# Memory keys, memory norm and state updates moved to other stages of a decoder step

## The chip, the cores and the metric

The kernel runs on one core of a Trainium2 chip. The metric is the device time of one launch in microseconds (us). An engine is named as in the profile: PE is TensorE's matmul and PEld its weight load, DVE is VectorE, ACT is ScalarE, POOL is GpSimd, and SP is the engine that issues most loads. L1134 is line 1134 of the kernel before.

## The reference, cut to what matters

One decoder layer is run for a prompt of 512 tokens and for a sample group of 8 sequences with 8 new tokens each; the 576 tokens share the weights. All is float32, with a model width of 2048.

```python
h = rms_norm(x, n_pre_mix)
rq, rk, rv, rg, dq, dk, dv = split(h @ w_in)
ret_o, ret_s = retention_chunked(rotate(rq), rotate(rk) * RET_DK ** -0.5, rv, ret_s0)   # S = gamma S + k^T v
diff_o = diff_attend(dq, keys, vals, ...)
mix = concat(silu(rg) * head_rms_norm(ret_o), head_rms_norm(diff_o)) @ w_out
x = x + rms_norm(mix, n_post_mix)
# cross attention: 4 heads of 128 over 256 memory tokens
mem_n = rms_norm(mem_prompt, norm_mem)           # 256 x 2048, prompt group only
mk_p, mv_p = mem_n @ w_xk, mem_n @ w_xv          # the sample group has cached keys and values
x = x + rms_norm(softmax((rms_norm(x, n_pre_x) @ w_xq) @ mk.T / sqrt(128)) @ mv @ w_xo, n_post_x)
h = rms_norm(x, n_pre_ffn)
x = x + rms_norm((silu(h @ w_gate) * (h @ w_up)) @ w_down, n_post_ffn)
```

The outputs are the new x, the new keys and values, the memory keys and values of the prompt, and the updated retention state of every sample (8 heads of 8 times 128 x 128, 4 MB).

## The kernel before

Activations lie transposed: 16 tiles of 128 features by 576 tokens. A float32 product is made of three matmuls in a rounded format: a high and a low part are split off each operand (`split`, L96 to L109: a copy on ACT, a subtraction on DVE), and high*high, high*low and low*high are added in PSUM (`mm3`). Weights come in pieces of 128 x 1024 (512 KB) through a ring of three raw tiles (`wraw`) and are split into rings of two (`wsplit`); products in w_in, w_out and the FFN follow Strassen's scheme over pairs of output blocks and have a second ring of three raw tiles (`w2`, tag wraw2).

The stages follow one another: w_in (8 to 441 us), retention and differential attention, w_out (to 1146), w_xq (1160 to 1215), cross attention (to some 1317), w_xo (to 1375), the FFN. Between w_out and w_xq, and between w_xo and the FFN, stands a norm: the sum of squares over all features is needed before the next operand can be scaled. `bcast_rstd` makes the scale: matmuls with a column of ones (rsb_pr), a root on ACT, a reciprocal and a product with the identity on DVE, matmuls that spread the result over the partitions (rsb_ps), and two copies. `prep_b1` (L1174) then makes each w_xq operand: a product on DVE (L1177), an addition of x by an accumulating DMA from POOL (L1181), a split, a store of the new x, a square and a sum into acc2 (L1189). Its source tiles xr lie in the slots `XS`, that is OAL 0 to 7 and OBH 0 to 7 of a grid of operand slots (7 names by 8 stages, 128 x 576 each).

The order on each engine is not that of the program text: a planner simulates the timeline and gives each engine a fixed queue, in which work that it expects to be ready runs ahead. So loads are hoisted as far as their buffers are free (the first two state loads, L1328, are issued at 1153.7, ahead of the projection). At run time each queue is served in order.

The memory is handled by `prep_mem` (L1131) and `mem_block` (L1146). `prep_mem` loads 16 tiles memT (128 features by 256 memory tokens, 128 KB) into the eight slots of OBL, splits each into a slot of XS as the x tiles there are used up, and squares and sums them (macc) for the memory norm. `mem_block(j)` is one block of 128 output columns: 16 feature tiles by 3 matmuls, 48 in all, then a product with the scale mrs; j 0 to 3 are the keys of the four heads and j 4 to 7 the values, which are also transposed. `cross_sample` works on two samples at a time (scores, softmax, product with the cached values), `cross_prompt(h)` on one head of the prompt, and `state_update(h)` on the retention state of one head: it loads the keys and values kvd (64 KB) and the state (512 KB), spreads the values with a mask (vbd), makes four matmul records (ru), adds on DVE (L1340) and stores. These are called in turn, so that matmul blocks stand between the softmaxes. `prep_bias` (L438) is an earlier example of small work set between two pairs of w_in.

Of the kernel before, what the change touches and what calls it, by code (L numbers as in the profile page):

```python
# [14 lines left out]
F32 = mybir.dt.float32  # L15
F32R = mybir.dt.float32r
# [32 lines left out]
def step_kernel(ctx: ExitStack, tc: tile.TileContext, a: dict, o: dict):  # L49
# [3 lines left out]
    def act(out, in_, func, **kw):  # L53
        S.activation(out, in_, func, **kw)  # L54
# [172 lines left out]
    def opslot(op, st):  # L227
        return op * 8 + st
# [129 lines left out]
    with ExitStack() as pha:  # L358
# [76 lines left out]

        br8d = dp.tile([8, BW], F32, name="br8d")

        def prep_bias():  # L438
            row = e1.w2("brow")[:8, :BW]
            p0, p1 = fb1("bp0"), fb1("bp1")  # L440
            TE.matmul(p0[:8], rb33, ohp[:, :512], start=True, stop=True)
            TE.matmul(p1[:8, : BW - 512], rb33, ohp[:, 512:], start=True, stop=True)
            act(row[:, :512], p0[:8], AF.Copy)
            act(row[:, 512:], p1[:8, : BW - 512], AF.Copy)
            SY.dma_start(br8d, row)
            for h in range(8):
                SY.dma_start(biasd[h], br8d[h : h + 1, :].to_broadcast([P, BW]))
# [676 lines left out]

        return mk

    macc = m0p.tile([P, NMEM], F32, name="macc")
    mrs = m0p.tile([P, NMEM], F32, name="mrs")
    mact = []

    def prep_mem():  # L1131
        for k in range(KT):
            mt = slot(opslot(OBL, k % 8), f"mt{k}")
            SY.dma_start(mt[:, :NMEM], a["memT"][k])  # L1134
            mhl = slot(XS[k], f"mhl{k}", F32R)[:, : 2 * NMEM].rearrange("p (i n) -> p i n", i=2)
            split(mhl[:, 0, :], mhl[:, 1, :], mt[:, :NMEM], gains[:, GMEM + k : GMEM + k + 1])
            mact.append(((mhl[:, 0, :], mhl[:, 1, :]),))
            if k == 0:
                act(macc, mt[:, :NMEM], AF.Square)
            else:  # L1140
                act(mt[:, NMEM : 2 * NMEM], mt[:, :NMEM], AF.Square)
                V.tensor_tensor(macc, macc, mt[:, NMEM : 2 * NMEM], ALU.add)

    mkT, mvn = [], []

    def mem_block(j):  # L1146
        po = pd.tile([P, 2, 512], F32, tag="d", name=f"mem{j}")[:, 0, :NMEM]
        for kh in range(2):
            ws = wload(a["w_mem"][j, kh], f"mem{j}_{kh}")
# [3 lines left out]
        t = m0p.tile([P, NMEM], F32, tag=f"mk{j}" if j < 4 else "mvt", name=f"mkv{j}")  # L1153
        V.tensor_tensor(t, po, mrs, ALU.mult)
        S.dma_start(o["memT"][j], t)
        if j < 4:
            mkT.append(t)
        else:
            pv = bank(f"mvt{j}")
            for i in range(2):  # L1160
                TE.transpose(pv[:, i * P : (i + 1) * P], t[:, i * P : (i + 1) * P], ident)
            vn = m0p.tile([P, NMEM], F32, name=f"mvn{j}")
            act(vn, pv[:, :NMEM], AF.Copy)
            mvn.append(vn)

    def add_dram(y, src, direct):
        if direct:
# [62 lines left out]
    cll = [opslot(op, st) for st in (0, 7) for op in range(4)] + [opslot(OBL, st) for st in range(8)]  # L1230
    cti = [0, 0]

    def cl(name):
# [84 lines left out]
            pt2[:, : 2 * P].rearrange("p (j h t) -> p j h t", j=2, h=XH)[:, :, :, 0:8],  # L1318
        )

    bdm = m0p.tile([NS, NB // 2], F32, name="bdm")
    SY.dma_start(bdm, a["bdm"])

    def state_update(h):
        kv = m0p.tile([NS, 2 * P], F32, tag="kvs", name=f"kvs{h}", bufs=2)
        SY.dma_start(kv, kvd[:, h, :])
        s0 = m0p.tile([P, NB * P], F32, tag="s0", name=f"s0_{h}", bufs=2)
        SY.dma_start(s0, a["state"][h].rearrange("p b v -> p (b v)"))  # L1328
        vbd = m0p.tile([NS, 512], F32, tag="vbd", name=f"vbd{h}", bufs=2)
        V.tensor_tensor(  # L1330
            vbd.rearrange("p (b v) -> p b v", b=4),
            kv[:, P:].unsqueeze(1).to_broadcast([NS, 4, P]),
            bdm.unsqueeze(2).to_broadcast([NS, 4, P]),
            ALU.mult,
        )
        pu = pd.tile([P, 2, 512], F32, tag="d", name=f"ru{h}")
        for g in range(2):
            rows = slice(32 * g, 32 * g + 32)
            TE.matmul(pu[:, g, :], kv[rows, :P], vbd[rows], start=True, stop=True)
        V.scalar_tensor_tensor(  # L1340
            s0, s0, (1.0 - 2.0 ** (-5.0 - h)) ** 8, pu.rearrange("p g n -> p (g n)"), ALU.mult, ALU.add
        )
        S.dma_start(o["rets"][h].rearrange("p b v -> p (b v)"), s0)

    def cross_prompt(h):
        ps = pd.tile([P, 2, 512], F32, tag="d", name=f"xs{h}")
        for qb in range(4):
# [53 lines left out]
    state_update(7)
    dsq = m0p.tile([P, 1], F32, name="dsq")
    act(dsq, epst, AF.Sqrt)
    for h in range(XH):
# [19 lines left out]
    def ydst(j):  # L1424
        yx[j] = slot(yslot[j], f"yx{j}") if j in yslot else w2(f"yx{j}")[:, :T]
        return yx[j]

    mk = post_evac(ydst, acc3, GQX)
    for j in range(KT):
        outs, parts = dpair(f"xo_{j}")  # L1430
        if j % 2 == 0:
            ws = wload(a["w_xo"][j // 2], f"xo{j}")
        for k in range(XH):
            i = (j % 2) * 4 + k
            mm3(outs, (ws[0][:, i, :], ws[1][:, i, :]), oxs[k], k == 0, k == XH - 1)
# [482 lines left out]
```

## Time and profile before

| | |
|---|---|
| time, median of 3 runs | 2946.92 us (2944.44 to 2948.87) |
| the profiled execution | 2941.53 us, its span 2939.5 us |
| busy: PE, DVE, ACT, POOL | 96%, 76%, 45%, 9% of the span |
| DMA | 493.62 MB, 168 GB/s over the span |
| chain that ended last | PE 83%, DMA 7%, DVE 5%, issue 3%, ACT 2% |

Busy time is the share of the span in which an engine had an instruction; matmuls overlap, so a busy PE need not run at its peak. PEclk is the granted TensorE clock, 1.00 being 2.4 GHz and 0.50 being 1.2 GHz. The chain is followed back from the last instruction, at each step to what released it. In a list in order of time, the bracket behind a row says how long the engine stood idle before it and what ended the wait.

### The profile page before, as it was taken

The numbers are of one execution on the slowest core, as the hardware profiler recorded it, in microseconds if no ns is written. First come the engines' busy times: TensorE is split into PE (matmuls) and PEld (weight loads), VectorE is DVE, ScalarE is ACT, GpSimd is POOL, SyncE is SP. The second block draws the span as 40 slices with busy tenths as digits, with TensorE's granted clock in tenths as the row PEclk, the third lists the DMA queues.
The fourth block names the chain that finished last, engine by engine and source line by source line (L and its number), as shares of the span: only waits on it lengthen the run. The fifth ranks groups of instructions, "written<-read, shape, count | busy, mean of one in ns | idle before, by whom it ended". The sixth has DMA issues, their size and how long they took to land.

```text
span 2939.5 us, 54583 instructions
## 1 busy us (share of the span) xinstructions
PE 2809.1 (96%) x22060; PEld 2710.6 (92%) x22060; DVE 2221.1 (76%) x3523; ACT 1333.4 (45%) x2183; POOL 252.9 (9%) x267
## 2 busy tenths in 40 slices
PE   8999998999999998998899999999999999999996
PEld 8899998888878998877799999999999999999995
DVE  8677767556555876864988888888888877888987
ACT  7333344444455645535744444444444444333441
POOL 0000003323332011000100000000000000000004
PEclk9999999999999999999999999999999999999998
DMA  5433336667664536863634444444444466455531
GB/s 166 150 117 126 119 126 240 240 212 256 219 235 163 176 118 214 275 222 96 178 128 140 132 154 133 142 143 137 149 143 131 149 231 228 158 203 207 180 115 65
DMA packets 203351, 493.62 MB, mean 168 GB/s; under 512 B 25907, under 2 KB 68403, under 8 KB 203100
## 3 DMA queue, kind: packets, MB, share of 16 engines
q1 hardware_dynamic: 122588, 334.14, 34.7%
q0 software_dynamic: 22464, 75.38, 8.1%
q10 hardware_dynamic: 58048, 80.63, 7.7%
q8 instruction: 173, 2.83, 0.4%
q14 instruction: 78, 0.64, 0.1%
HBM read 407.07 MB, written 85.61 MB: 168 GB/s over the span
## 4 chain that ended last, share of the span: by engine, by line
PE 83%; DMA 7%; DVE 5%; issue 3%; ACT 2%; POOL 1%; SPq 0%; ACTq 0%; DVEq 0%; POOLq 0%
PE dX L1624 9%; PE Yg L307 7%; PE Yu L307 7%; PE Yin L307 5%; PE Zg L307 5%; PE Xu L307 4%; PE Zu L307 4%; PE Xg L307 4%; PE dZ L1624 4%; PE Xin L307 3%; PE Zin L307 3%; PE rk L118 2%; PE dY L1624 2%; PE Ywo L307 2%; PE rv L118 2%
## 5 line engine op out<-in xcount | busy, mean ns | idle before, releaser
L1624 PE MATMUL dX<-fo,wd 128*128 128x288 f32 x1872 | 271.0, 296 | 4.0 <-ACT ysl L54 4.0
L1624 PEld LDWEIGHTS dX<-fo,wd 128*128 128x128 f32 x1872 | 257.1, 189 | 4.2 <-ACT ysl L54 4.2
L54 ACT ACTIVATE wd<-wr_d 128x512 fp32r<-128x512 f32 x156 | 97.5, 630 | 119.3 <-PE dX L1624 56.7
L1624 PE MATMUL dZ<-fo,wd 128*128 128x288 f32 x936 | 139.2, 294 | 0.0
L1744 POOL TENSOR_TENSOR fin<-fin,ysq 128x320 f32<-128x320 f32 (+1 forms) x10 | 8.4, 839 | 1467.5 <-ACT ysq L54 1467.5
L1624 PEld LDWEIGHTS dZ<-fo,wd 128*128 128x128 f32 x936 | 129.2, 188 | 0.0
L106 DVE TENSOR_TENSOR wd<-wr_d,wd 128x512 fp32r<-128x512 f32 x156 | 106.4, 687 | 12.5 <-ACT wd L54 12.0
L54 ACT ACTIVATE wd<-d 128x512 fp32r<-128x512 f32 x78 | 48.9, 631 | 75.8 <-PE dZ L1624 40.1
L1624 PE MATMUL dY<-fo,wd 128*128 128x288 f32 x468 | 75.5, 295 | 0.0
L698 POOL DMA_INDIRECT vu<-cv,idx x64 | 62.8, 981 | 102.5 <-PE ou L790 62.4
L698 POOL DMA_INDIRECT ku<-ck,idx x64 | 63.7, 996 | 77.5 <-PE su L729 46.7
L54 ACT ACT_TABLE_LOAD x51 | 65.4, 1283 | 9.8 <-DVE ms L1258 2.3
L307 PE MATMUL Xg<-op,wh_p1g 128*128 128x288 f32 x336 | 67.7, 296 | 0.0
L307 PE MATMUL Xu<-op,wh_p1u 128*128 128x288 f32 x336 | 67.6, 296 | 0.0
L1624 PEld LDWEIGHTS dY<-fo,wd 128*128 128x128 f32 x468 | 66.7, 188 | 0.0
L106 DVE TENSOR_TENSOR wd<-d,wd 128x512 fp32r<-128x512 f32 x78 | 53.5, 689 | 9.9 <-ACT wd L54 9.4
L328 DVE TENSOR_TENSOR w_s1g<-w_a21g,wr_a22g 128x1024 f32<-128x1024 f32 x21 | 25.7, 1225 | 40.8 <-DMA w_a21g<-w_gate 40.8
L307 PE MATMUL Yg<-oph,wh_p6g 128*128 128x288 f32 x168 | 50.6, 301 | 5.0 <-ACT oph L54 5.0
L118 PE MATMUL mem<-mhl,wh_mem 128*128 128x256 f32 x256 | 51.5, 298 | 3.1 <-DVE mp L1258 1.9
L307 PEld LDWEIGHTS Xu<-op,wh_p1u 128*128 128x128 f32 x336 | 53.9, 188 | 0.0
L307 PEld LDWEIGHTS Xg<-op,wh_p1g 128*128 128x128 f32 x336 | 53.9, 188 | 0.0
L307 PE MATMUL Xin<-op,wh_p1in 128*128 128x288 f32 x256 | 51.6, 296 | 0.0
(1153 smaller groups left out, 10923.3 us busy)
## 6 DMA issues: line engine op xcount, KB each, us to landing
fo<-fo SPq DMA_DIRECT2D x140, 288.0 KB
wr_d<-w_down SPq DMA_DIRECT2D x39, 512.0 KB
d<-w_down SPq DMA_DIRECT2D x39, 512.0 KB
fo<-sh ACTq DMA_DIRECT2D x60, 288.0 KB
fo<-sl ACTq DMA_DIRECT2D x60, 288.0 KB
w_a21g<-w_gate SPq DMA_DIRECT2D x21, 512.0 KB
wr_a11g<-w_gate SPq DMA_DIRECT2D x21, 512.0 KB
wr_a22g<-w_gate SPq DMA_DIRECT2D x21, 512.0 KB
```

The source lines that it names most:

```text
L54: S.activation(out, in_, func, **kw)
L106: V.tensor_tensor(lo, src, hi.bitcast(F32), ALU.subtract)
L118: TE.matmul(po, ws, x[h][xi], start=start and i == 0, stop=stop and i == 2)
L307: TE.matmul(bk[:, :HN], w[wx][:, st, :], ops[op][st][xi], start=first and st == 0 and i == 0, stop=st == 7 and i == 2, skip_group_check=True,)
L328: V.tensor_tensor(s1, a21, a22, ALU.add)
L698: G.indirect_dma_start(t, None, src, bass.IndirectOffsetOnAxis(ap=idx[:, pg : pg + 1], axis=0))
L1624: TE.matmul(bk[:, :HN], w[wi][:, st, :], ops[e][st][xi], start=start and st == 0 and i == 0, stop=st == 3 and i == 2, skip_group_check=True,)
L1744: (V if j % 2 == 0 or j > 11 else G).tensor_tensor(ac[:, hs], ac[:, hs], sq, ALU.add)
```

## The change

The keys leave `mem_block`. They become a group in eight chunks (`mem_k_chunk`) between w_out and the w_xq projection: each chunk loads 512 KB of weights for two feature tiles and all four heads, two memT tiles, splits both, and adds 24 matmuls into two PSUM banks (kb), which stay taken until two copies (kraw) at the end. The row scale of x (`bcast_rstd`, rsb1) stands between the second and the third chunk. The memT tiles pass through two buffers (tag mt). Their split tiles lie for k 0 to 7 in two tags of two buffers each (b12, tt) and for k 8 to 15 in the slots of OBL, where they stay for the values. For the values, `prep_mem` loads and splits k 0 to 7 a second time: the raw tile into a slot of OBH (`XS[8 + k % 6]`), the split one into OAL.

The squares of the memory norm come from a second, natural copy of the memory in w_in, behind the third pair of blocks: four tiles of 512 KB through the ring `w2`, a square with a running sum on ACT, and root and reciprocal into mstd. `mem_k` spreads it by one product and one matmul and scales the keys.

The state updates leave the cross attention. Heads 0 to 3 stand behind blocks 4, 7, 10 and 13 of w_xo; heads 4 and 5 inside, heads 6 and 7 behind the `bcast_rstd` of the gap behind w_xo. State tiles are halved (256 KB), kvd comes for two heads at a time, and all lie in operand slots. The cached tiles of `cross_sample` rotate over 14 slots (OBH 0 to 5 instead of OBL 0 to 7).

```diff
+        def prep_mem_sums():
+            ms = fa.tile([P, 4], F32, name="ms")
+            for i in range(4):
+                t = e1.w2(f"mn{i}")
+                SY.dma_start(t, a["memN"][i // 2][:, (i % 2) * 1024 : (i % 2 + 1) * 1024])
+                act(t, t, AF.Square, accum_out=ms[:, i : i + 1])
+            msv = ms.rearrange("p (i c) -> p i c", c=2)
+            V.tensor_tensor(mstd, msv[:, :, 0], msv[:, :, 1], ALU.add)
+            act(mstd, mstd, AF.Sqrt, scale=1.0 / D, bias=epst)
+            V.reciprocal(mstd, mstd)
...
+            if n == 2:
+                prep_mem_sums()
...
-    bcast_rstd(acc1, rsb, D, T, "rsb1", fb2)
+    kraw = [slot(opslot(OBH, 6 + i), f"kraw{i}")[:, :512] for i in range(2)]
+    kb = [fb2(f"memk{i}") for i in range(2)]
+    mact = [None] * KT
+
+    def mem_split(k, mt, t):
+        mhl = t[:, : 2 * NMEM].rearrange("p (i n) -> p i n", i=2)
+        split(mhl[:, 0, :], mhl[:, 1, :], mt, gains[:, GMEM + k : GMEM + k + 1])
+        mact[k] = ((mhl[:, 0, :], mhl[:, 1, :]),)
+
+    def mem_k_chunk(c):
+        ws = wload(a["w_mem_g"][c], f"memk{c}")
+        for k in (2 * c, 2 * c + 1):
+            mt = y1p.tile([P, NMEM], F32, tag="mt", name=f"mt{k}", bufs=2)
+            SY.dma_start(mt, a["memT"][k])
+            if k < 8:
+                t = fb.tile([P, T], F32R, tag=("b12", "tt")[k % 2], name=f"mhl{k}", bufs=2)
+            else:
+                t = slot(opslot(OBL, k % 8), f"mhl{k}", F32R)
+            mem_split(k, mt, t)
+        for k in (2 * c, 2 * c + 1):
+            for j in range(4):
+                wi = 2 * j + k % 2
+                for i, (wx, xi) in enumerate(((0, 0), (0, 1), (1, 0))):
+                    TE.matmul(
+                        kb[j // 2][:, (j % 2) * NMEM : (j % 2 + 1) * NMEM],
+                        ws[wx][:, wi, :],
+                        mact[k][0][xi],
...
+    for c in range(KT // 2):
+        if c == 2:
+            bcast_rstd(acc1, rsb, D, T, "rsb1", fb2)
+        mem_k_chunk(c)
+    for i in range(2):
+        act(kraw[i], kb[i], AF.Copy)
     ph2.close()
...
     def prep_mem():
-        for k in range(KT):
-            mt = slot(opslot(OBL, k % 8), f"mt{k}")
-            SY.dma_start(mt[:, :NMEM], a["memT"][k])
-            mhl = slot(XS[k], f"mhl{k}", F32R)[:, : 2 * NMEM].rearrange("p (i n) -> p i n", i=2)
-            split(mhl[:, 0, :], mhl[:, 1, :], mt[:, :NMEM], gains[:, GMEM + k : GMEM + k + 1])
-            mact.append(((mhl[:, 0, :], mhl[:, 1, :]),))
-            if k == 0:
-                act(macc, mt[:, :NMEM], AF.Square)
-            else:
-                act(mt[:, NMEM : 2 * NMEM], mt[:, :NMEM], AF.Square)
-                V.tensor_tensor(macc, macc, mt[:, NMEM : 2 * NMEM], ALU.add)
+        for k in range(8):
+            mt = slot(XS[8 + k % 6], f"mtv{k}")[:, :NMEM]
+            SY.dma_start(mt, a["memT"][k])
+            mem_split(k, mt, slot(XS[k], f"mhlv{k}", F32R))
...
+    mem_k()
     prep_mem()
-    bcast_rstd(macc, mrs, D, NMEM, "mrs")
...
     cross_sample(0)
     cross_sample(2)
-    mem_block(0)
     mem_block(4)
     cross_prompt(0)
-    state_update(0)
     cross_sample(4)
-    mem_block(1)
-    state_update(1)
     mem_block(5)
     cross_prompt(1)
...
+    RS0 = [opslot(op, st) for st in (1, 2, 3) for op in range(5)] + [opslot(OAL, 4)]
+    def state_update(h, bk):
+        if h % 2 == 0:
+            kvt2[0] = slot(opslot(OBL, h // 2), f"kvs{h}")[:NS, :512].rearrange("p (h c) -> p h c", h=2)
+            SY.dma_start(kvt2[0], kvd[:, h : h + 2, :])
+        kv = kvt2[0][:, h % 2, :]
+        vbd = slot(opslot(OBH, h % 4), f"vbd{h}")[:NS, :512]
...
+        for g in range(2):
+            s0 = slot(RS0[2 * h + g], f"s0_{h}_{g}")[:, :512]
+            SY.dma_start(s0, a["state"][h][:, 4 * g : 4 * g + 4, :].rearrange("p b v -> p (b v)"))
+            rows = slice(32 * g, 32 * g + 32)
+            pu = bk(f"ru{h}_{g}")
+            TE.matmul(pu, kv[rows, :P], vbd[rows], start=True, stop=True)
+            V.scalar_tensor_tensor(s0, s0, (1.0 - 2.0 ** (-5.0 - h)) ** 8, pu, ALU.mult, ALU.add)
+            S.dma_start(o["rets"][h][:, 4 * g : 4 * g + 4, :].rearrange("p b v -> p (b v)"), s0)
...
         mk(j)(parts)
+        if j in (4, 7, 10, 13):
+            state_update((j - 4) // 3, bank)
...
+    def fbank_ru(name):
+        if name == "rsb2_ps0":
+            state_update(4, fbank)
+            state_update(5, fbank)
+        return fbank(name)
+
+    bcast_rstd(acc3, rsf, D, T, "rsb2", fbank_ru)
+    state_update(6, fbank)
+    state_update(7, fbank)
```

## Rows read from the trace of the kernel before

**Rows 1.** The page, part 1: engines, busy us over the span.
```profile
PE 2809.1 (96%) x22060; PEld 2710.6 (92%) x22060; DVE 2221.1 (76%) x3523; ACT 1333.4 (45%) x2183; POOL 252.9 (9%) x267
```

**Rows 2.** Busy us by stretch: PE, PEld, DVE, ACT, POOL; granted clock, DMA share, GB/s.
```profile
1146.20:1215.20 69.00, 55.64 (x390) 53.42 (x391) 55.13 (x88) 42.69 (x76) 12.43 (x15) 0.90 0.99 287
1215.20:1317.20 102.00, 92.64 (x743) 75.52 (x742) 67.12 (x113) 43.37 (x97) 0.00 (x0) 0.95 0.68 229
1317.20:1374.90 57.70, 56.05 (x398) 54.26 (x396) 22.27 (x26) 27.05 (x40) 0.00 (x0) 0.97 0.27 91
1374.90:1421.00 46.10, 30.39 (x200) 27.82 (x199) 34.91 (x59) 32.40 (x55) 12.13 (x14) 0.85 0.80 194
```

**Rows 3.** TensorE in order of time, first gap (start, us; in brackets its wait).
```profile
1149.20 1.18 PE L179 MATMUL rsb_pr<-ones,acc 128*96 128x1 f32 x12 [3.00 <-DVE acc L1062]
1153.75 2.29 PE L203 MATMUL rsb_ps<-rsb,ones 96*128 96x288 f32 x4 [3.37 <-DVE rsb L190]
1160.62 1.33 PE L118 MATMUL xq<-h2h,wh_xq 128*128 128x288 f32 x4 [4.57 <-ACT h2h L54]
```

**Rows 4.** Busy times in steps of 2 us, same gap.
```profile
1162.00:1164.00 2.00, 2.00 (x10) 2.00 (x10) 2.00 (x4) 1.14 (x2) 0.67 (x2) 0.50 0.77 175
1164.00:1166.00 2.00, 2.00 (x16) 2.00 (x15) 1.89 (x3) 0.00 (x0) 1.48 (x2) 0.95 0.98 146
```

**Rows 5.** Chain of waits, memory blocks (start, us, what).
```profile
1226.19 5.75 PE mem L118 x47
```

**Rows 6.** State update: its matmuls in the chain, then tiles vbd and s.
```profile
1239.38 1.06 PE ru L1339 x4
...
L1330 DVE TENSOR_TENSOR vbd<-kvs,bdm x8: 682/684/687, 1157.0 to 1306.5; 64x512 f32<-64x512 f32 x8
...
L1340 DVE SCALAR_TENSOR_TENSOR s<-s,ru x8: 1210/1214/1222, 1240.5 to 1318.3; 128x1024 f32<-128x1024 f32 x8
```

**Rows 7.** Tiles mt and wr_mem: instructions (ns least/median/most, first and last start).
```profile
L54 ACT ACTIVATE mhl<-mt,gains x16: 492/494/510, 1169.8 to 1218.6; 128x256 fp32r<-128x256 f32 x16
L109 DVE SCALAR_TENSOR_TENSOR mhl<-mt,gains,mhl x16: 476/480/485, 1173.4 to 1219.2; 128x256 fp32r<-128x256 f32 x16
...
L54 ACT ACTIVATE wh_mem<-wr_mem x16: 1041/1059/1065, 1214.7 to 1302.5; 128x1024 fp32r<-128x1024 f32 x16
L96 DVE TENSOR_TENSOR wl_mem<-wr_mem,wh_mem x16: 1214/1225/1227, 1216.2 to 1303.6; 128x1024 fp32r<-128x1024 f32 x16
```

**Rows 8.** Chain of waits, single loads.
```profile
1186.79 9.30 DMA mt<-memT
...
1215.67 3.30 DMA xvc<-cmv
```

**Rows 9.** SP's issues of memT, and ScalarE's wait for them.
```profile
1147.25 1.70 SPq L1134 DMA_DIRECT2D mt<-memT  x2
...
1153.59 0.76 ACT L54 ACTIVATE mt<-mt 128x256 f32<-128x256 f32 x2 [1.12 <-DMA mt<-memT]
```

**Rows 10.** Chain of waits, w_xo.
```profile
1330.02 44.80 PE xo L118 x334
```

**Rows 11.** VectorE in order of time, behind the projection.
```profile
1217.76 0.75 DVE L1189 TENSOR_TENSOR acc<-acc,xr 128x576 f32<-128x576 f32 x1
...
1231.57 0.19 DVE L1211 COPY xqs<-xq 128x64 f32<-128x64 f32 x1
```

**Rows 12.** TensorE in order of time, cross attention.
```profile
1259.98 0.69 PE L1315 MATMUL yt<-ident,yob 128*128 128x128 f32 x2 [2.33 <-DVE yob L1312]
```

**Rows 13.** All engines in order of time, the gap behind w_xo.
```profile
1378.03 1.15 PE L179 MATMUL rsb_pr<-ones,acc 128*96 128x1 f32 x12 [2.96 <-ACT yx L54]
...
1381.88 2.29 PE L203 MATMUL rsb_ps<-rsf,ones 96*128 96x288 f32 x4 [2.70 <-DVE rsf L190]
...
1389.96 0.61 PE L118 MATMUL gu0a<-op,wh_gu 128*128 128x288 f32 x1 [5.79 <-ACT op L54]
```

**Rows 14.** Busy times by stretch, w_in.
```profile
100.00:120.00 20.00, 17.35 (x109) 15.57 (x108) 7.54 (x7) 6.53 (x9) 0.00 (x0) 0.91 0.53 160
```

More of the change, by code (lines that the diff above doesn't have):

```diff
@@ L69, in step_kernel @@
     SY.dma_start(gains, a["gains"])
+    mstd = cp.tile([P, 2], F32, name="mstd")
     mixd = dp.tile([KT, P, T], F32, name="mixd")
@@ L1125, in post_evac, with mem_k @@
         return mk
-    macc = m0p.tile([P, NMEM], F32, name="macc")
     mrs = m0p.tile([P, NMEM], F32, name="mrs")
-    mact = []
     def prep_mem():
-        for k in range(KT):
-            mt = slot(opslot(OBL, k % 8), f"mt{k}")
-            SY.dma_start(mt[:, :NMEM], a["memT"][k])
-            mhl = slot(XS[k], f"mhl{k}", F32R)[:, : 2 * NMEM].rearrange("p (i n) -> p i n", i=2)
-            split(mhl[:, 0, :], mhl[:, 1, :], mt[:, :NMEM], gains[:, GMEM + k : GMEM + k + 1])
-            mact.append(((mhl[:, 0, :], mhl[:, 1, :]),))
-            if k == 0:
-                act(macc, mt[:, :NMEM], AF.Square)
-            else:
-                act(mt[:, NMEM : 2 * NMEM], mt[:, :NMEM], AF.Square)
-                V.tensor_tensor(macc, macc, mt[:, NMEM : 2 * NMEM], ALU.add)
-    mkT, mvn = [], []
+        for k in range(8):
+            mt = slot(XS[8 + k % 6], f"mtv{k}")[:, :NMEM]
+            SY.dma_start(mt, a["memT"][k])
+            mem_split(k, mt, slot(XS[k], f"mhlv{k}", F32R))
+    mkT, mvn = [], []
+    def mem_k():
+        V.tensor_tensor(
+            mrs.rearrange("p (c j) -> p c j", c=2),
+            ident.unsqueeze(1).to_broadcast([P, 2, P]),
+            mstd.unsqueeze(2).to_broadcast([P, 2, P]),
+            ALU.mult,
+        )
+        pb = bank("mrs_ps")
+        TE.matmul(pb[:, :NMEM], ones, mrs, start=True, stop=True)
+        act(mrs, pb[:, :NMEM], AF.Copy)
+        for j in range(4):
+            t = m0p.tile([P, NMEM], F32, tag=f"mk{j}", name=f"mkv{j}")
+            V.tensor_tensor(t, kraw[j // 2][:, (j % 2) * NMEM : (j % 2 + 1) * NMEM], mrs, ALU.mult)
+            S.dma_start(o["memT"][j], t)
+            mkT.append(t)
     def mem_block(j):
@@ L1148, in mem_block @@
         for kh in range(2):
-            ws = wload(a["w_mem"][j, kh], f"mem{j}_{kh}")
+            ws = wload(a["w_mem"][j - 4, kh], f"mem{j}_{kh}")
             for k8 in range(8):
@@ L1152, in mem_block @@
                 mm3([(po, 0)], (ws[0][:, k8, :], ws[1][:, k8, :]), mact[k], k == 0, k == KT - 1)
-        t = m0p.tile([P, NMEM], F32, tag=f"mk{j}" if j < 4 else "mvt", name=f"mkv{j}")
+        t = m0p.tile([P, NMEM], F32, tag="mvt", name=f"mkv{j}")
         V.tensor_tensor(t, po, mrs, ALU.mult)
         S.dma_start(o["memT"][j], t)
[L1156 to L1164, printed above, removed]
+        pv = bank(f"mvt{j}")
+        for i in range(2):
+            TE.transpose(pv[:, i * P : (i + 1) * P], t[:, i * P : (i + 1) * P], ident)
+        vn = m0p.tile([P, NMEM], F32, name=f"mvn{j}")
+        act(vn, pv[:, :NMEM], AF.Copy)
+        mvn.append(vn)
     def add_dram(y, src, direct):
@@ L1225, in step_kernel @@
     )
+    mem_k()
     prep_mem()
-    bcast_rstd(macc, mrs, D, NMEM, "mrs")
     ctl = [opslot(op, st) for st in (1, 2, 3, 6) for op in range(4)]
-    cll = [opslot(op, st) for st in (0, 7) for op in range(4)] + [opslot(OBL, st) for st in range(8)]
+    cll = [opslot(op, st) for st in (0, 7) for op in range(4)] + [opslot(OBH, st) for st in range(6)]
     cti = [0, 0]
@@ L1319, in cross_sample @@
         )
[L1321 to L1343, printed above, removed]
     def cross_prompt(h):
@@ L1858 @@
     )
+    wk = n["w_xk"][0]
+    A["w_mem_g"] = _wgroup([wk[:, j * P : (j + 1) * P] for j in range(4)], nat)
+    A["memN"] = np.ascontiguousarray(n["mem_prompt"][0].reshape(2, P, D))
     A["w_out"] = _wblocks(n["w_out"][0])
-    A["w_mem"] = _wblocks(np.concatenate([n["w_xk"][0], n["w_xv"][0]], 1))
+    A["w_mem"] = _wblocks(n["w_xv"][0])
     A["w_gate"] = _wblocks(n["w_gate"][0])
```

22 lines of the change are left out of this document (13 added, 9 removed).

## The prediction

> **What bounds the kernel now.** I read the page's busy times first, then the busy times by stretch, then the waits of TensorE one by one, and only then single transfers. TensorE is busy for 2809.1 of 2939.5 us [rows 1], so whatever the change brings has to come out of some 130 us in which it stands idle, or out of stretches at the lower clock. By stretch [rows 2], two pieces between w_out and the first FFN product are poor: from 1146.2 to 1215.2 (gap behind w_out, then the w_xq group) TensorE works 55.6 of 69.0 us at a granted clock of 0.90, and from 1374.9 to 1421.0 (the gap behind w_xo) 30.4 of 46.1 us at 0.85. The cross-attention stretch in between works 92.6 of 102.0 us, and w_xo itself 56.1 of 57.7 us.
>
> The waits say what the first gap is [rows 3]: w_out's products end at 1146.2 (1149.2 less its wait), then TensorE waits 3.0 us for the sum of squares, 3.4 us for the row scale and 4.6 us for the first normed operand; the projection starts at 1160.6. The granted clock falls to its lower level, 0.50 (1.2 GHz), after these waits and is back only in 1164 to 1166 [rows 4], so the first 3.5 us of the projection run at half speed. In the same stretch DMA is the full resource: a mean busy share of 0.99 over 69 us [rows 2]. So the gap is cheap for TensorE work whose operands have been loaded, and a bad place for work that must be loaded there. That is the question of this change.
>
> I make the sum against the profiled execution, 2941.5 us (span 2939.5 and 2.0 around it). The median of the runs shown is 2946.9, 5.4 above; I add that at the end.
>
> **What leaves the cross stretch.** A block of memory keys is 48 matmuls; 47 took 5.75 us [rows 5], 0.122 us each, 5.9 us a block, 23.4 us for four. One state update takes 1.06 us of TensorE [rows 6]. Eight leave this stretch; four go into w_xo, where TensorE has no room (56.1 of 57.7), so they only change place; the other four, 4.2 us, go into the last gap. Together 27.6 us leave. The memory norm's squares and sums leave VectorE and ScalarE there too; I count nothing for that, because TensorE's work is what covers them.
>
> **What the keys cost in their new place.** Eight chunks, 24 matmuls or 2.9 us each. Chunks 0 and 1 can be split before w_out ends: their memT tiles fit the two mt buffers in turn and the w_out queue is light. Chunk 2's memT tiles wait, loaded, for chunk 0's split tiles (two of each tag), so they are split at about 1146.2 + 2.9 + 1.4 = 1150.5. From there on every chunk needs two new memT tiles through the same two buffers: issue, landing, a 0.49 us copy on ScalarE, a 0.48 us subtraction on VectorE [rows 7], and only then the next issue. I call the landing L and put 1.5 us on the rest. The chunk period is L + 1.5, against 2.9 us of matmuls, and SP issues in order, so every load queued behind a waiting memT load waits as well. In before, eight buffers held these tiles, so this ring is new.
>
> L is bounded on both sides by single transfers. Just behind the projection 256 KB landed in 3.30 us; in the loaded projection a memT tile took 9.30 us [rows 8]. Nearer in place: two issued from 1147.3 were used at 1153.6, at most 6.3 us [rows 9]. I take 3.3: while the ring paces SP, SP has little else in flight, and the accumulating x transfers start only behind the row scale. The Trainium skill (DMA: Bandwidth & Descriptors, Anatomy of one DMA — SWDGE path) gives about 2.0 us plus the bytes over 436 GB/s, by which 128 KB is an estimated 2.3 us, and the sum below would come out 5 us lower; the rows here lie above it, and no run shows the loaded case of the new order.
>
> With 3.3 the period is 4.8: the last of five chunks starts at 1150.5 + 24.0 = 1174.5 and ends at 1177.4. The projection is 384 matmuls of 0.133 us (w_xo's steady rate, [rows 10]), 51 us; I let 4 us of it run in the pauses of the ring, on the PSUM banks that the keys don't hold. It then ends at 1224.4 instead of 1215.2: **+9.2**. From below: with the keys dense (23.4) and the scale's own 1.8 us beside them it ends at 1222.3, +7.1. From above: L = 9.3 makes the period 10.8, the keys end at 1207.4, and with 10 us of the projection pulled forward it ends at 1248: +33.
>
> Beside the ring, the rest of this group hides. A chunk's weights take 1.06 us on ScalarE and 1.23 us on VectorE [rows 7] in a ring of two, so they are ready 2.3 us behind the chunk before last, inside the 2.9 us of the chunk between; without that cover (a dense group) it would be some 0.5 us a chunk. The row scale is asked for behind chunk 1, when its sum (acc1, VectorE at 1149) is just there; its matmuls then run between key chunks, and VectorE's and ScalarE's splits, 2.2 and 2.0 us a chunk, can push it back by one instruction, 1.2 us, which is inside the keys' time. The two raw copies at the end are one more ScalarE pass each, before the keys are needed by 20 us; the scale of the keys is now one matmul on a finished column. SP gets eight memT loads more (0.33 us each to issue, 1 MB), behind the xr loads and ahead of the cross-attention tiles; POOL's queue gets nothing.
>
> **A late start of the values.** The change splits k 0 to 7 a second time, and loads mt for k = 5 into the slot of xr 13, which is read until the last sum of acc2. That sum starts at 1217.8, 2.6 us behind the projection [rows 11]. Then come 3.3 us of transfer and 1 us of split: some 7 us, against about 4 us of work (five k of the first value block, the rsx matmuls). In before only the split stood there. **+3**, between 0 and 5.
>
> **Less cover.** Key blocks filled TensorE while the xq scale was made (the last xqs copy is at 1231.6, 16 us behind the projection, [rows 11]) and between softmaxes. Even with eight blocks TensorE waited 2.3 us for VectorE at one place [rows 12]. With four blocks fewer such waits are hidden. Four cross_sample and four cross_prompt chains are left with half the cover; at half a us each: **+4**; 0 if the remaining blocks suffice, 13 if six of them show some 2.2 us each.
>
> **The last gap.** Four updates bring 4 times 0.68 us of VectorE for vbd, which can be made early in w_xo (VectorE 22 of 58 us busy there), and 4 times 1.21 us for the state [rows 6]. Their matmuls fit TensorE's waits of 3.0, 2.7 and 5.8 us [rows 13]. But VectorE runs in order, and the chain to the first FFN matmul runs through it (the row scale, the ym products and sums). Of 4.9 us I put **+1.5** on the path; at best −0.5, as work in the gap keeps the clock up; at worst all 4.9, with 2 MB of state writes beside a stretch that DMA fills to 0.80 [rows 2].
>
> **The memory sums.** Four 512 KB tiles pass through the three-buffer ring that feeds the w_in products, each with a squaring of about 1.06 us. When prep_bias went through there, TensorE worked 17.4 of 20 us [rows 14]. **+1**, between 0 and 4.
>
> Sum: −27.6 + 9.2 + 3 + 4 + 1.5 + 1 = −8.9; 2941.5 − 8.9 = 2932.6, and with 5.4 added 2938.
>
> **Rivals.** (A) The ring decides, slower: L as in the loaded projection, 9.3 us. Then −27.6 + 33 + 3 + 4 + 1.5 + 1 = +15, 2962. It turns from gain to loss where the projection ends 18 us late, at a period of 6.6, L = 5.1; the 6.3 us of [rows 9] lie above that, the 3.3 of [rows 8] below. For it: DMA at 0.99 in this stretch. Against it: SP, held by the ring, can't prefetch cross-attention tiles, which were part of that load.
> (B) Cover, no change: cross attention becomes a chain of softmaxes and gives 13 us back: about 2947. For it the wait in [rows 12]; against it, 92.6 of 102 us busy. That the planner's order puts keys behind the projection after all, so that the gap stays, ends here too.
> (C) The gap fills as meant: dense keys, no late values, no loss elsewhere: −27.6 + 7.1 = −20.5, 2926.
>
> **How the numbers follow.** The forecast (2933 to 2943) has 0.37, C 0.19, B 0.22, A 0.22. A measurement of this kernel can tell about 0.2%, 5.9 us, from no change. Faster by more: most of the forecast, 0.33, and C, 0.19: 0.52. Slower: A less its mild end, and a worse B: 0.22. Within: 0.26. The range, 2922 to 2960, runs from a little below C to just under A's full price, and leaves out about 1 in 10 on either side.
>
> **What would show it.** Right: key matmuls between 1146 and about 1177, a granted clock that stays at 1.0, the projection ending near 1224, w_xo ending some 13 us earlier than 1374.9, the FFN's first matmul about 15 us behind it as before. Wrong: single key chunks 7 us or more apart, each behind a memT landing (A); the cross stretch little shorter than 102 minus 15 us, with TensorE waiting for VectorE (B); a wait of 3 us or more in w_in behind a squaring; the state sums between the scale and ym in the last gap.

## The result, and the profile after

The changed kernel takes 2971.31 us (median of 4 runs, 2968.87 to 2974.14), the kernel before 2946.43 us on the same chip (4 runs, 2944.44 to 2948.87): a ratio of 1.0084, 95% interval 1.0067 to 1.0102. It is **slower by 0.84%**; forecast were 2938 us and a range of 2922 to 2960. The spans of the two profiled executions, 2939.5 and 2967.1 us, differ by 27.6 us, and the stages below are read from these two. A profiled execution can lie some 5 us to either side of its kernel's median (before 5 below it, experiment e1 4 above), so stage differences of 2 or 3 us are not taken for effects.

The page, part 1, answers to [rows 1]: busy us over the span.

```profile
PE 2832.6 (95%) x22056; PEld 2727.7 (92%) x22056; DVE 2219.1 (75%) x3524; ACT 1339.9 (45%) x2188; POOL 252.9 (9%) x267
```

TensorE has four matmuls fewer and is busy for 23 us longer. The same matmuls ran longer: that points to the clock. The same stages as in [rows 2] (keys, projection, cross attention, w_xo, gap and first 32 us of the FFN), columns as there:

```profile
1155.10:1216.00 60.90, 34.67 (x211) 32.05 (x209) 46.63 (x68) 36.80 (x58) 12.42 (x15) 0.75 0.91 242
1216.00:1267.40 51.40, 51.40 (x373) 51.40 (x374) 18.06 (x24) 14.77 (x21) 0.00 (x0) 0.96 0.60 197
1267.40:1337.70 70.30, 60.89 (x514) 47.91 (x512) 38.88 (x74) 30.08 (x74) 0.00 (x0) 0.93 0.54 180
1337.70:1399.40 61.70, 60.76 (x416) 54.80 (x414) 32.27 (x49) 29.83 (x50) 0.00 (x0) 1.00 0.44 148
1399.40:1447.40 48.00, 40.15 (x229) 33.14 (x229) 38.73 (x65) 32.45 (x55) 12.12 (x14) 0.82 0.86 231
```

From the end of w_out to the start of the projection it was 14.4 us (1146.2 to 1160.6); it is now 60.9 us, of which TensorE works 34.7. The projection itself went from 54.6 to 51.4 us, cross attention from 102.0 to 70.3, w_xo (to the end of its last matmul, 1375.1 and 1399.4) from 57.9 to 61.7, the last gap from 15.0 to 16.1 (to the first FFN matmul at 1415.5). What moved out of cross attention did come out. What came in behind w_out costs more than that.

The keys stretch in steps of 5 us, to be held against [rows 4], same columns:

```profile
1165.00:1170.00 5.00, 4.98 (x38) 4.54 (x37) 4.46 (x9) 3.19 (x5) 0.18 (x1) 1.00 0.65 222
1170.00:1175.00 5.00, 1.09 (x8) 0.68 (x6) 5.00 (x8) 3.57 (x8) 0.98 (x1) 1.00 0.60 196
1175.00:1180.00 5.00, 4.31 (x22) 4.10 (x22) 3.05 (x6) 0.99 (x3) 1.77 (x2) 0.66 1.02 234
1180.00:1185.00 5.00, 1.28 (x5) 0.99 (x6) 5.00 (x8) 4.54 (x8) 1.72 (x2) 0.71 1.01 218
...
1190.00:1195.00 5.00, 0.00 (x0) 0.00 (x0) 2.35 (x4) 2.30 (x3) 0.79 (x1) 0.73 1.05 265
1195.00:1200.00 5.00, 3.74 (x15) 3.45 (x16) 4.25 (x7) 3.30 (x6) 1.73 (x2) 0.50 0.79 189
```

Two halves. Up to about 1170.5 four and a half chunks (108 of the 192 key matmuls, nine memT tiles) run dense, at a granted clock of 1.00 in the last full slice. By then the row scale is ready (1168.3), the preparation of x starts (POOL's column is no longer near zero, DMA goes to about 1.0), and TensorE alternates between idle and work; the granted clock of these slices is 0.50 to 0.74, between its two levels or at the lower one.

TensorE's waits from 1100 to 1460 us, by line and releaser (us in all, times, longest), which answer to [rows 3, 12]:

```profile
PE memk L1137 <- ACT mhl L54: 12.5, 4, 6.6
PE memk L1137 <- DVE mhl L110: 7.9, 4, 3.1
PE xq L119 <- ACT kraw L54: 5.8, 1, 5.8
PE xs L1379 <- DVE mkv L1200: 4.3, 1, 4.3
```

The waits of [rows 3] for the row scale and the first operand are gone, as the change set out to do. In their place stand 20.4 us for split memory tiles and 5.8 us for the copy that frees the keys' banks. Which of a tile's steps was late is read from the issues, engine by engine. SP's queue (start, duration):

```profile
1174.90 1.09 SPq L1127 DMA_DIRECT2D mt<-memT  x2
1183.93 0.33 SPq L90 DMA_DIRECT2D wr_xq<-w_xq_g  x1
1184.36 1.36 SPq L1127 DMA_DIRECT2D mt<-memT  x2
1195.97 0.33 SPq L90 DMA_DIRECT2D wr_xq<-w_xq_g  x1
1197.03 0.33 SPq L1127 DMA_DIRECT2D mt<-memT  x1
```

ScalarE's (in brackets its wait and what ended it):

```profile
1179.14 0.77 ACT L54 ACTIVATE h2h<-ym,gains 128x576 fp32r<-128x576 f32 x1 [4.01 <-DMA ym<-xT]
...
1181.34 0.89 ACT L54 ACTIVATE mhl<-mt,gains 128x256 fp32r<-128x256 f32 x2
...
1191.84 0.78 ACT L54 ACTIVATE h2h<-ym,gains 128x576 fp32r<-128x576 f32 x1 [3.39 <-DMA ym<-xT]
...
1195.27 0.51 ACT L54 ACTIVATE mhl<-mt,gains 128x256 fp32r<-128x256 f32 x1 [1.14 <-DMA mt<-memT]
...
1197.21 0.51 ACT L54 ACTIVATE mhl<-mt,gains 128x256 fp32r<-128x256 f32 x1 [1.43 <-DMA mt<-memT]
```

VectorE's subtractions, which end a split and free the buffer:

```profile
1183.82 0.48 DVE L110 SCALAR_TENSOR_TENSOR mhl<-mt,gains,mhl 128x256 fp32r<-128x256 f32 x1
...
1196.53 0.48 DVE L110 SCALAR_TENSOR_TENSOR mhl<-mt,gains,mhl 128x256 fp32r<-128x256 f32 x1
```

And three landings, of the loads issued at 1174.90, 1184.36 and 1185.39 (KB, us from issue to landing):

```profile
mt<-memT SPq DMA_DIRECT2D x1, 128.0 KB, 4.4
...
mt<-memT SPq DMA_DIRECT2D x1, 128.0 KB, 10.9
...
mt<-memT SPq DMA_DIRECT2D x1, 128.0 KB, 11.8
```

Two rounds of the ring, late for two reasons. In the first, a tile issued at 1174.90 lands at 1179.3, but ScalarE copies it only at 1181.34, behind an operand of x that had itself waited 4.01 us for a transfer, and VectorE subtracts at 1183.82; only then can the next load be issued, at 1184.36: 9.5 us, of which the landing is 4.4 and the rest 5.1. In the second, the tile is copied at 1195.27, as soon as it lands, and the next load goes out at 1197.03: 12.7 us, of which the landing is 10.9 and the rest 1.8. With two tiles a round, TensorE begins on them at 1171.9, 1181.9, 1195.8 and 1204.1: periods of 10.0, 13.9 and 8.3 us, 10.7 in the mean, where rival A had 10.8. The transfers issued from 1171 to 1208, behind the row scale (KB each, median us from issue to landing over those whose landing the trace tells, for memT the three above), answering to [rows 8, 9]:

```profile
x1d<-ym ACTq DMA_DIRECT2D x12, 288.0 KB, 5.0
ym<-xT POOLq DMA_DIRECT2D x12, 288.0 KB, 7.2
wr_xq<-w_xq_g SPq DMA_DIRECT2D x4, 512.0 KB
mt<-memT SPq DMA_DIRECT2D x5, 128.0 KB, 10.9
```

and two pieces of the chain that ended last (start, us, what):

```profile
1185.39 11.80 DMA mt<-memT
...
1206.68 7.98 DMA ym<-xT
```

The chain changes between memT and x transfers: neither waits alone.

### The profile page after: what moved, and what is told of

Read it like the earlier page. It is cut to its first block, busy times and chain, and to the rows that moved or that the text cites. A ratio compares the mean times of both kernels' runs of the same rounds, so it can differ in the third digit from the quotient of the medians.

```text
span 2967.1 us, 54638 instructions
## 1 busy us (share of the span) xinstructions
PE 2832.6 (95%) x22056; PEld 2727.7 (92%) x22056; DVE 2219.1 (75%) x3524; ACT 1339.9 (45%) x2188; POOL 252.9 (9%) x267
## 4 chain that ended last, share of the span: by engine, by line
PE 83%; DMA 6%; DVE 5%; issue 3%; ACT 2%; POOL 1%; SPq 0%; ACTq 0%; DVEq 0%; POOLq 0%
PE dX L1679 9%; PE Yu L308 7%; PE Yg L308 7%; PE Yin L308 5%; PE Zg L308 5%; PE Xu L308 4%; PE Zu L308 4%; PE Xg L308 4%; PE dZ L1679 4%; PE Xin L308 3%; PE Zin L308 3%; PE rk L119 3%; PE dY L1679 2%; PE Ywo L308 2%; PE rv L119 2%
## 5 line engine op out<-in xcount | busy, mean ns | idle before, releaser
L107 DVE TENSOR_TENSOR wd<-wr_d,wd 128x512 fp32r<-128x512 f32 x156 | 106.3, 686 | 11.6 <-ACT wd L54 10.9
L54 ACT ACT_TABLE_LOAD x53 | 68.0, 1283 | 18.4 <-DVE ms L1313 10.9
L308 PE MATMUL Yg<-opl,wh_p6g 128*128 128x288 f32 x168 | 50.7, 302 | 1.7 <-DVE opl L107 1.7
```

What stands on the lines that cost most here:

```text
L107: V.tensor_tensor(lo, src, hi.bitcast(F32), ALU.subtract)
L308: TE.matmul(bk[:, :HN], w[wx][:, st, :], ops[op][st][xi], start=first and st == 0 and i == 0, stop=st == 7 and i == 2, skip_group_check=True,)
```

## The experiments

Times differ from chip to chip and from group to group (2943.6, 2952.6 and 2945.5 us for the kernel before in the three groups e1 to e4, e5 to e8, e9 to e12), so kernels are compared by their ratio to the kernel before in their own group. "Keys" is the time from the first to the last key matmul, and "to the projection's end" the time from w_out's end: 69.0 us before, 112.3 after.

**e1: memT four tiles at a time, in three buffers.**

```diff
+        if c % 2 == 0:
+            mt4[0] = e3.w2(f"mt{c}").rearrange("p (k n) -> p k n", k=4)
+            SY.dma_start(mt4[0], a["memT"][2 * c : 2 * c + 4].rearrange("k p n -> p k n"))
         for k in (2 * c, 2 * c + 1):
-            mt = y1p.tile([P, NMEM], F32, tag="mt", name=f"mt{k}", bufs=2)
-            SY.dma_start(mt, a["memT"][k])
+            mt = mt4[0][:, k % 4, :]
```

> The changed kernel with one edit: the memT tiles of the keys come four at a time into the three free tiles of the w2 ring (512 KB each), so no chunk waits for a two-buffer ring. Theory R (the two-buffer ring and the landing of each memT tile make the keys last 55 us instead of 25): the keys become dense, about 25 to 30 us behind w_out, the projection ends some 30 us earlier than in the changed kernel, and the time is 2936 to 2943. Theory O (the x operands, whose preparation starts behind the second chunk, stand ahead of the memT splits in the queues of ScalarE and VectorE, and wait there for accumulating transfers): ScalarE still waits for x in front of the splits, the keys stay above 45 us, and the time stays within 10 us of 2971.

Measured: 0.9971 (0.9953 to 0.9988), faster than before and 1.1% faster than the changed kernel. The transfers, and the first key matmuls, first and last start behind the durations (ns least/median/most):

```profile
mt<-memT SPq DMA_DIRECT2D x4, 512.0 KB, 8.0
```

```profile
L1141 PE MATMUL memk<-mhl,wh_memk x128: 274/283/415, 1155.7 to 1184.4; 128*128 128x256 f32 x128
```

The larger transfer landed in 8.0 us (the one of four whose landing the trace tells), but all four were issued by 1148.6, before w_out ended, and no key matmul waited for a split memory tile. Keys take 28.9 us in place of 54.7, to the projection's end it is 83.9. The x preparation starts at 1170 as in the changed kernel, beside the keys. The run changes the size of a load, the number of buffers and the time of issue at once; e6 goes back to single loads.

**e2: the call for the row scale behind all chunks.**

```diff
-        if c == 2:
-            bcast_rstd(acc1, rsb, D, T, "rsb1", fb2)
...
+    bcast_rstd(acc1, rsb, D, T, "rsb1", fb2)
     ph2.close()
```

> The changed kernel with one edit: the row scale of x stands behind all eight chunks, not behind the second, so nothing of x is prepared during the keys; the two-buffer ring stays. Theory R: a memT tile still needs its landing of some 4 us and the split of 1.5 us, so the last five chunks take about 5.5 us each, the keys some 40 us, then the gap of 14 us comes behind them: the time stays at 2965 to 2975. Theory O: the keys take under 30 us, the projection starts some 42 us behind w_out instead of 61, and the time falls to about 2952.

Measured: 1.0085 (1.0065 to 1.0105), the changed kernel's time. But the scale's matmuls stood where they had stood, at 1162.7 and 1168.1, 5.7 and 11.1 us behind the first key matmul (changed kernel: 5.7 and 11.1): the planner puts work where its operands are ready, and the place of the call in the text moved nothing. This run separates nothing; e5 does it by a dependency.

**e3 and e4: one part of the change alone, in the kernel before.** e3 moves only the state updates, e4 only the squares of the memory norm.

```diff
-    state_update(0)
...
+        if j in (4, 7, 10, 13):
+            state_update((j - 4) // 3, bank)
...
+    bcast_rstd(acc3, rsf, D, T, "rsb2", fbank_ru)
```

> The kernel before with only the state updates moved (into w_xo and the last gap). Theory of the ledger: eight updates of 1.06 us leave the cross stretch, w_xo grows by 4, the last gap by 1 and the first FFN group by 2: about 1.5 us faster, not to be told from before. Rival: without their cover the cross stretch gives back half, 2 to 4 us slower.

```diff
+            if n == 2:
+                prep_mem_sums()
...
-                act(mt[:, NMEM : 2 * NMEM], mt[:, :NMEM], AF.Square)
-                V.tensor_tensor(macc, macc, mt[:, NMEM : 2 * NMEM], ALU.add)
```

> The kernel before with only the memory norm's sums from natural rows in w_in; memT tiles are loaded and split as before, without their squares and sums. Theory of the ledger: w_in ends 4.4 us later, for the four tiles in the ring of weights, and nothing comes back: 3 to 5 us slower. Rival: 15 squares and 15 sums less beside the projection and one scale less behind it give the 4 us back: no change.

Measured: e3 0.9979 (0.9967 to 0.9992), some 6 us faster; e4 1.0001 (0.9989 to 1.0014), no difference, though in its profile the attention starts 3.9 us later than before. Neither part by itself makes the kernel slower; that leaves the keys.

**e5: the row scale made to wait for the keys**, by adding zero times a key to its sum.

```diff
-        if c == 2:
-            bcast_rstd(acc1, rsb, D, T, "rsb1", fb2)
...
+    for i in range(2):
+        V.scalar_tensor_tensor(acc1[:, i : i + 1], kraw[i][:, 0:1], 0.0, acc1[:, i : i + 1], ALU.mult, ALU.add)
+    bcast_rstd(acc1, rsb, D, T, "rsb1", fb2)
```

> The changed kernel with the row scale of x behind the keys by a true dependency: two columns of the sum acc1 get the raw keys times 0.0 added, so nothing of x can be prepared before the keys end (moving the call alone left the order of the queues as it was). The two-buffer ring stays. Theory R (ring and landing): without the x transfers a landing falls from 4.7 us to about 3.5, a chunk period to about 5, so the keys take some 35 us instead of 55, and the gap and the projection (14 + 55) follow in full: projection end near 1260, time 2960 to 2968. Theory O (x work in the same queues is the whole of it): keys under 30 us, projection end near 1254, time 2952 or less.

Measured: 1.0024 (1.0009 to 1.0039). The ring of two is still there, nothing of x is; the keys:

```profile
L1137 PE MATMUL memk<-mhl,wh_memk x128: 274/283/387, 1164.6 to 1195.8; 128*128 128x256 f32 x128
```

31.3 us, which is what the forecast had for the ring (1146.2 to 1177.4); SP issues the last rounds of loads at 1176.9, 1181.8, 1185.9 and 1190.5, that is 4.2 to 4.9 us apart, and the forecast's period was 4.8. The gap of before then follows them, and the projection's end comes 98.8 us behind w_out. So the ring of two costs little by itself: 2.4 us over e1.

**e6: memT singly, but in three buffers.**

```diff
-            mt = y1p.tile([P, NMEM], F32, tag="mt", name=f"mt{k}", bufs=2)
+            mt = e3.w2(f"mt{k}")[:, :NMEM]
```

> The changed kernel with the memT tiles, still one by one, in the three tiles of the w2 ring instead of a ring of two; x is prepared as in the change. Theory R: a chunk's period falls to two thirds, the keys from 55 to about 40 us, the time to 2950 to 2958. Theory O: nothing changes, 2965 to 2975.

Measured: 0.9998 (0.9984 to 1.0012). The keys:

```profile
L1137 PE MATMUL memk<-mhl,wh_memk x128: 274/283/504, 1165.4 to 1193.2; 128*128 128x256 f32 x128
```

Keys 27.9 us, to the projection's end 86.4. One more buffer does nearly all that e1 does, more than expected. x starts where it did in the changed kernel, 16 us behind the first key matmul, but the last memT load is out 20 us behind it (1185.2), in the changed kernel 42 us (1197.0): few loads are left to meet x's.

**e7 and e8: e1, with the squares in smaller tiles outside the weights' ring (e7), and then one of the two key copies on VectorE (e8).**

```diff
-                t = e1.w2(f"mn{i}")
-                SY.dma_start(t, a["memN"][i // 2][:, (i % 2) * 1024 : (i % 2 + 1) * 1024])
+                t = t576(f"mn{i}")[:, :512]
+                SY.dma_start(t, a["memN"][i // 4][:, (i % 4) * 512 : (i % 4 + 1) * 512])
```

> The kernel of e1_wide_mt with the squares of the memory norm on eight 256 KB tiles of the t576 ring instead of four in the ring of weights. If the 4 us that w_in lost are the ring of weights, they come back: 2931 to 2934. If they are ScalarE's time and the transfers, 2935 to 2938.

```diff
-        act(kraw[i], kb[i], AF.Copy)
+        (act(kraw[i], kb[i], AF.Copy) if i else V.tensor_copy(kraw[i], kb[i]))
```

> e7_wide_sums_t576 with one of the two copies of the raw keys on VectorE instead of ScalarE, so that the projection's banks come free together. If the wait of 2.1 us for these copies counts, 1 to 2 us less than e7; VectorE's queue holds x work too, so it may be no change.

Measured: e7 0.9971 (0.9959 to 0.9983), e1's own ratio, and w_in still ends at 444.8 in place of 441.7. One execution is thin evidence for 3 us, but the others agree: in the eleven profiles with the squares in w_in the first matmul behind it starts at 443.4 to 448.2, in the three without them at 441.7 to 443.2. So the ring of weights isn't what w_in loses its 3 to 4 us to. e8 0.9988 (0.9973 to 1.0003): no gain from the copy.

**e9 and e10: which side of x hurts the ring.** In e9 x's transfers move the same bytes but no operand waits for them; in e10 they are gone, while the other work on x and its stores stay.

```diff
-            G.dma_start(y, a["xT"][k], accum_op=ALU.add)
+            G.dma_start(dums[k % 4], a["xT"][k], accum_op=ALU.add)
```

> The changed kernel with the 14 accumulating transfers of x going into four idle tiles, so that the operands of w_xq are made without waiting for them (x is left out of 14 of the 16 sums; the transfers, the stores and the engine work all stay). It parts two ways in which x's preparation can stretch the ring of two. Theory L (landing: the traffic itself makes each memT tile land late): the keys stay at 45 us or more. Theory Q (queue: the memT splits stand on ScalarE behind operands that wait for their x): the keys fall to 35 us or less.

```diff
-        else:
-            G.dma_start(y, a["xT"][k], accum_op=ALU.add)
```

> The changed kernel without the 14 accumulating transfers (x is left out of 14 of the 16 sums); the stores of x1d and all engine work stay. Either theory expects keys of 28 to 34 us, near the 31 us of the run in which x's preparation is held back; if the keys stay above 40 us, engine work of x in the queues, not its transfers, is the cause.

Measured: e9 1.0073 (1.0050 to 1.0095), keys 58.5 us; e10 1.0032 (1.0015 to 1.0049), keys 45.5 us:

```profile
L1137 PE MATMUL memk<-mhl,wh_memk x128: 274/283/582, 1152.1 to 1210.4; 128*128 128x256 f32 x128
...
L1137 PE MATMUL memk<-mhl,wh_memk x128: 274/283/582, 1154.7 to 1200.1; 128*128 128x256 f32 x128
```

TensorE's waits in e9, then two of ScalarE's:

```profile
PE memk L1137 <- ACT mhl L54: 14.3, 4, 7.0
PE memk L1137 <- DVE mhl L110: 9.5, 4, 3.9
```

```profile
1179.58 0.51 ACT L54 ACTIVATE mhl<-mt,gains 128x256 fp32r<-128x256 f32 x1 [3.22 <-DMA mt<-memT]
1182.20 0.51 ACT L54 ACTIVATE mhl<-mt,gains 128x256 fp32r<-128x256 f32 x1 [2.11 <-DMA mt<-memT]
```

and its memT transfers issued from 1171 to 1208 (the landing is told for two of the five, 10.0 and 9.5 us):

```profile
mt<-memT SPq DMA_DIRECT2D x5, 128.0 KB, 9.8
```

The splits shown stand behind no waiting operand; they wait for memT itself, which lands about as late as in the changed kernel's second round. So the keys can be as long without any wait of x for its transfers on ScalarE. What such a wait costs in the changed kernel (4.01 us in its first round) this run doesn't tell, since its transfers and stores lie closer together. In e10, TensorE's waits, its memT transfers issued from 1171 to 1200 (told for two of five, 3.4 and 4.2 us), and VectorE in order of time:

```profile
PE memk L1137 <- DVE mhl L110: 11.2, 5, 3.5
...
PE memk L1137 <- ACT mhl L54: 1.4, 1, 1.4
```

```profile
mt<-memT SPq DMA_DIRECT2D x5, 128.0 KB, 3.8
```

```profile
1190.35 0.47 DVE L110 SCALAR_TENSOR_TENSOR mhl<-mt,gains,mhl 128x256 fp32r<-128x256 f32 x1
1190.74 0.74 DVE L1232 TENSOR_TENSOR ym<-xr,rsb 128x576 f32<-128x576 f32 x1
1191.41 0.80 DVE L110 SCALAR_TENSOR_TENSOR h2l<-ym,gains,h2h 128x576 fp32r<-128x576 f32 x1
1192.14 0.74 DVE L1242 TENSOR_TENSOR acc<-acc,xr 128x576 f32<-128x576 f32 x1
1192.81 0.47 DVE L110 SCALAR_TENSOR_TENSOR mhl<-mt,gains,mhl 128x256 fp32r<-128x256 f32 x1
```

memT now lands in 3.8 us, near the 3.3 of the forecast, and yet the keys take 14 us longer than in e5: the second split of a chunk stands behind three instructions on x in VectorE's fixed queue, and every split holds back the next load. So traffic is one part, x's own engine work another.

**e11: e1 with the state updates back in cross attention.**

```diff
     cross_prompt(0)
+    state_update(0)
     cross_sample(4)
+    state_update(1)
...
-        if j in (4, 7, 10, 13):
-            state_update((j - 4) // 3, bank)
```

> The kernel of e1_wide_mt with the state updates as in the kernel before, in the cross stretch: the key group and the sums alone. The state move alone gave 0.9979 and e1 0.9971 of before. If the two add up, the keys without a ring are worth 0.1%, and this is 0.999 of before. Rival: the state updates are welcome cover where the keys have left, and this is as fast as e1, 0.997.

Measured: 1.0019 (1.0005 to 1.0032). Moving the updates is worth 0.2% in the kernel before (e3), and 0.5% where the keys have left cross attention (e1 against e11). The keys are as dense here (1152.8 to 1182.3), but the projection takes 59.8 us in place of e1's 52.6 and waits 4.3 us for its weights' low part.

**e12: e1 with the squares behind the second pair of w_out**, in eight 256 KB tiles.

```diff
-            if n == 2:
-                prep_mem_sums()
...
             post_out(2 * n + i, t)
+        if n == 3:
+            prep_mem_sums()
```

> The kernel of e1_wide_mt with the squares of the memory norm in w_out (behind its second pair of blocks, eight tiles of 256 KB in the t576 ring) instead of w_in. If the 4 us that w_in lost are the sums', they come back, as w_out's DMA is at 0.4: 0.9955 to 0.996 of before. Rival: they are lost in w_out instead, 0.997.

Measured: 0.9954 (0.9940 to 0.9968), 2932.3 us: the best of all, faster than both kernels. The first matmul behind w_in, of the changed kernel and of e12 (first start behind the durations):

```profile
L119 PE MATMUL rq<-oph,wh_rq x48: 290/295/401, 446.1 to 623.5; 128*128 128x288 f32 x48
```

```profile
L119 PE MATMUL rq<-oph,wh_rq x48: 292/295/609, 441.7 to 621.7; 128*128 128x288 f32 x48
```

w_in has its 441.7 us of before again. The interval still overlaps e1's, so the gain over e1 is likely rather than shown; in the two profiles e12's lead of 3.5 us behind w_in has shrunk to 1.1 us at the end of w_out (1154.8 against 1155.9), and what it gains behind that was not taken apart.

## Why the prediction was wrong

The sum of the forecast, term by term, beside the two profiled executions (us):

| step | forecast | measured |
|---|---|---|
| w_out's end to the projection's end | +9.2 | +43.3 (69.0 to 112.3) |
| out of cross attention, late values, less cover | -27.6 + 3 + 4 = -20.6 | -27.9 (cross -31.7, w_xo +3.8) |
| last gap | +1.5 | +1.1, and +2.0 in the FFN's first group |
| memory sums in w_in | +1 | +4.4 |
| attention, w_out | 0 | +2.2, +2.4 |
| sum | -8.9 | +27.5 |

**The step that failed** is the period of the ring, "The chunk period is L + 1.5": both of its terms were too small, and with them the keys.

The landing L: "I take 3.3: while the ring paces SP, SP has little else in flight, and the accumulating x transfers start only behind the row scale." Behind the row scale it measured 4.4, 10.9 and 11.8 us. Both halves of the sentence are true and don't carry the conclusion. SP's queue was light, but the traffic came from POOL's (12 transfers of x from 1171 to 1208) and ScalarE's (12 stores of x).

The rest: "put 1.5 us on the rest", that is on the copy, the subtraction and the next issue. It measured 5.1 us in the round issued at 1174.90, with x's work ahead of the split on ScalarE and VectorE, and 1.8 in the next. The forecast asked whether the splits push the row scale back; that x's work pushes the splits back it put at nothing. The row scale was ready at 1168.3, so x's work lay beside the second half of the keys. By e10 this term is the larger: the keys stay 14.2 us longer than in e5 although memT lands in 3.4 and 4.2 us.

Rival A named the ring and its turning point, a period of 6.6. That its own period, 10.8, stands so near the mean of 10.7 is in part luck: it had a landing of 9.3 in every round, where the rounds took 10.0, 13.9 and 8.3 us and the first of them landed in 4.4. Its keys would have ended 61.2 us behind w_out; they took 54.7, as four and a half chunks ran dense and not three. Its price, +33, was still 10 too low, for another step that failed: "I let 4 us of it run in the pauses" (10 in rival A). No projection matmul ran before 1216.0: the first waited 5.8 us for the copy that empties the keys' banks, which stood behind an operand of x on ScalarE.

The Trainium skill (DMA: Bandwidth & Descriptors, Anatomy of one DMA — SWDGE path) gave an estimated 2.3 us for 128 KB. The Trainium skill gives this fit for transfers that GpSimd issues; memT's are issued by SP. The least memT landing of the changed kernel, 2.2 us, agrees with it; the 4.4 to 11.8 us where x's transfers run beside it don't, and the measurement decides. The 5 us that the forecast would have taken off its sum by this estimate also go below its own floor for dense keys, +7.1 against the +9.2 of the sum.

**What the keys' 54.7 us are made of.** Without the ring's limit, x beside them: 28.9 (e1), 27.9 (e6). With the ring of two, x held back: 31.3 (e5). Ring and x's engine work, without x's transfers: 45.5 (e10). All: 54.7. In that order the ring by itself costs 2.4, x's engine work ahead of the splits 14.2, x's loads, by their traffic or by the waits for them, 9.2. Neither the ring nor x beside the keys does it alone: a late landing, or a split behind x, costs only where the next load waits for that buffer. This is shown by e1, e6 and e5. The split of the 23 us into engine work and loads rests on e10 alone, and on this order of taking things away. That e9, in which nothing waits for x's transfers, has still longer keys (58.5) fits transfers and stores closer together (they land in 9.8 and 9.7 us, 7.2 and 5.0 in the changed kernel), but was not taken apart. What w_in lost its 4 us to stays open as well: to the squares being there (e12), but not to the ring of weights (e7).

**What was right.** Cross attention lost 31.7 us; the keys and eight updates were forecast at 23.4 + 8.5 = 31.9, and four updates cost w_xo 3.8 (4.2). So the two charges on it, late values (+3) and less cover (+4), came to nothing in sum: TensorE stands idle for 9.4 us of this stretch in both kernels, now with one wait of 4.3 us for the scaled keys and none for a value block. Rival B did not happen. The projection took 51.4 (51). The gap behind w_xo took 1.1 us more (1.5). The ring's own 31.2 us came out at 31.3, and its period of 4.8 at 4.2 to 4.9, where x was held back (e5).

**What the change is worth, mended.** e3 0.9979, e1 0.9971, e12 0.9954. The state updates alone give 0.2%; e1, with dense keys and the squares in w_in as well, can't be told from that; and the keys and squares without the updates lose 0.2% (e11). So the two moves seem worth more together than one by one, which the intervals leave open, and that moving the keys adds anything to the updates alone is likely only in e12. Rival C had 7.1 us for the stretch up to the projection's end with dense keys; e1 needs 14.9 more than before (83.9 less 69.0): keys 28.9 rather than 25.2, a 2.1 us wait for their copy, a projection of 52.6.

## What to carry to other kernels

A landing time belongs to a stretch, not to a queue: take it from the stretch in which the transfer will run, with everything that the change lets start there, from all queues. The time from a landing to the next issue belongs to it as well: it is as long as what stands ahead of the split in the queues of the engines that make it. Where a ring has to be refilled in a loaded stretch, deepen it by one buffer or load ahead of the stretch; here a third buffer gave back 0.85%, and four tiles a transfer, loaded ahead, 1.1%. The count of what leaves a stage came out here to a microsecond while the price of its new place was off by thirty: put the doubt, and the chances, there.

## What was not expected of the hardware

The landing of a transfer went by what ran beside it more than by its size: 128 KB took 4.4 to 11.8 us beside x's loads and stores, 3.4 and 4.2 us beside the stores alone (e10), while a load of 512 KB ahead of them landed in 8.0 us in e1 and 4.2 us in e12. And in a chopped stretch the clock falls, as in [rows 4]: after the waits TensorE worked at a granted clock of 0.50 to 0.74, and 22 of the 24 matmuls of a pair of tiles, back to back, took 4.2 and 4.8 us (from 1174.9 and from 1197.1), where 0.122 us each, as in [rows 5], makes 2.7. Between two rounds the next wait covers this; it is paid where the waits end, in the first 4 us of the projection, at 0.55, in which 18 matmuls ran that take 2.4 us at 0.133 us each:

```profile
1216.00:1220.00 4.00, 4.00 (x18) 4.00 (x19) 1.80 (x3) 1.87 (x3) 0.00 (x0) 0.55 1.05 318
```
